# ScalarE takes over state copies, block copies, scaled products and gate biases in the mixers of a hybrid backbone block

## The chip, the cores and the metric

The kernel runs on one core of one Trainium2 chip. The metric is device microseconds of one execution, launch to end. Three runs of the kernel before gave a median of 1978.37 us (1975.06 to 1981.58).

Engines are named as the profile names them: PE is TensorE (PEld its weight loads), DVE is VectorE, ACT is ScalarE, POOL is GpSimd, SP issues most transfers. Each engine takes its instructions strictly in the order in which the program lists them for that engine, so an instruction that waits holds back all behind it on the same engine.

## The reference, cut to what matters

One layer, 256 latent tokens and 256 context tokens, width 2048, fp32. Each sequence is normalised and modulated, projected with `w_in`, and split into four head groups. Three of them are recurrences that run forward and backward; the context's end state starts the latent scan.

```
q, k = l2norm(q), l2norm(k)                                # GDN: 4 heads of 128
S_t = a_t (I - beta_t k_t k_t^T) S_{t-1} + beta_t k_t v_t^T ; o_t = S_t^T q_t
decay = exp(-c * sigmoid(w0 + tanh(w_lo) @ w2))            # RWKV-7: 8 heads of 64
a     = sigmoid(a0 + a_lo @ a2)
S_t = S_{t-1} (diag(w_t) - kk_t^T (a_t * kk_t)) + v_t^T k_t ; y_t = S_t r_t
```

The other two groups are GLA (a gated linear attention) and a short convolution. The four outputs are joined, multiplied by `w_out`, added to the stream; then a SwiGLU of width 5632 and a last RMSNorm on the latent tokens. The context goes through the mixers only, and of those through the recurrences' states only.

## The kernel before, in words

All is one core, four stages on the time axis of the profile:

- 0 to about 160 us: modulation vectors and the first projections (eleven tiles of `w_early`) for the context.
- about 160 to 1100 us: the mixers. The list `ORDER` names their pieces. Small letters are the context (`s == 0`), capitals the latent tokens (`s == 1`): `rw0` to `rw3` are RWKV head pairs (function `rwkv`, both directions `d`, so 16 unit passes in all), `gd0` to `gd3` are GDN heads (function `gdn`, eight passes), `gl` GLA pairs, `SC` short convolutions, and `pd`, `pr`, `pg` are projections whose results are parked in DRAM until a unit fetches them. Three further modulation vectors (`ada_pieces`, weights from `in_ada_later`) are fed in between the projections.
- about 1095 to 1240 us: `w_out` and the second norm. From there to the end: SwiGLU.

Every weight tile of a projection arrives as f32 (`wraw`). `split` makes from it a rounded part `wh` (ACT, line 197) and a rest `wl` (DVE, line 202); PE then multiplies three times (`wh` by the rounded activations, `wh` by their rest, `wl` by the rounded ones) into the PSUM tile `big`. The pool has three `wh` and three `wl`.

RWKV runs as stream "a", GDN and GLA as stream "b". Each unit pass has a front, a mid and a back part, and `in_parts` lets the front of the next pass run before the back of the last one. The two streams have PSUM tiles of their own: `ea` (two buffers) and `la` (one) for "a", `eb` (one) and `lb` (one) for "b".

The framework's planner works out, when the program is built, the order of instructions on each engine, from the order of the calls and from priorities: `tc.high_priority()` around a weight's load and split, and the offsets in `ORDER`. At run time that order is fixed.

The places that the change touches:

- `rw_gates` (line 837): two matmuls per pass (decay and `a`), each into an `ea` tile. DVE adds the bias and bounds from below by -87 in one instruction (line 847, recorded as helper line 208), into the halves of `rw_z`. ACT then makes the sigmoid of both halves in three instructions of 512 columns.
- `halves` (line 863): copies one block of 128 by 256 into a zero-filled block-diagonal tile `bd`, one instruction for each 64 partitions. `NB` and `KB` (from the two parts of `rw_BK`) go by DVE (line 873), `VB` by ACT (line 197).
- the state loop in the RWKV `back`: per chunk, PE forms `pS` and the output `po` in one `la` tile, and DVE multiplies `pS` by the chunk's decay into `rw_S` (helper line 206); for `d == 0` ACT copies `po`, for `d == 1` DVE adds it. There are 56 such states.
- GDN: the products `kk` and `kq` are copied out of an `eb` tile by DVE (lines 1145 and 1179); in `back`, each unit's product `pf` in the `lb` tile is scaled twice, by beta on ACT (`gd_Fb`, line 199) and by -beta exp(cum) on DVE (`gd_Fg`, line 206), two units per PSUM tile, and PE then multiplies with `gd_Fg`.

```
acopy(Fb[:, u]..., src, scale=sm["beta"][:, d, h, c:c + 1])
ts(Fg[:, u]..., src, sm["nbe"][:, d, h, c:c + 1], MUL)
```

Of the kernel before, what the change touches and what calls it, by code (L numbers as in the profile page):

```python
# [175 lines left out]
def block_kernel(ctx: ExitStack, tc: tile.TileContext, x, cx, ada_first, ada_later, ada_b, w_in, w_early, w_out,  # L176
# [63 lines left out]
    def pc(name, i=0, n=1, lo=0, hi=P):  # L240
        return par[lo:hi, POFF[name] + i:POFF[name] + i + n]
# [274 lines left out]
    with mix:  # L516
# [323 lines left out]
        def rw_gates(p, d, sm):  # L840

            z = mk(mx, [P, 2, T], "rw_z", 1)
            for i, n in enumerate(("w0", "a0")):
                pl = PB([P, T])
                w0 = i * 1024 + d * 512 + p * P
                mm(pl, sw[:, w0:w0 + P], sm["smd"][d])
                ts(z[:, i], pl, pc(n, d * 4 + p), ADD, -87.0, MAX)
            sigmoid(z.rearrange("p a t -> p (a t)"))
            cu = t1("rw_cu")
            runsum(cu, z[:, 0], d, z64)  # L850
            return cu, z[:, 1]
# [47 lines left out]
        def rwkv(p, s, raw, sm):  # L899
# [52 lines left out]
            def mid(d, v):  # L952
                cur[0] = "a"
                lo = 1 if d == 0 else 0
                KK, BK = v["KK"], v["BK"]
                NB, KB, VB = (r.next() for r in bd[1:])
                vv = t1("rw_v")
                shift(vv, com["v"], d * 12 + 8 + p, d)
                halves(NB, BK[:, :, 0, :], V)
                halves(KB, BK[:, :, 1, :], V)  # L960
                halves(VB, c64(vv), A)
                if s == 1:
                    r = t1("rw_r")
                    shift(r, com["r"], d * 12 + p, d)
                    IR = v["IR"] = mk(mx, [P, 4, 2, 64], "rw_IR", 1)
                    G.tensor_copy(IR[:, :, 0, :], bcast(istack, 1, 4))
                    tt(IR[:, :, 1, :], c64(r), v["ep"][:, :, lo:lo + 64], MUL)
                    rk = t1("rw_sq")
                    stt(rk, r, pc("rk", p), v["kp"], MUL, MUL)
                    pr = PB([P, T])  # L970
                    mm(pr, onesbd, rk)
                    if d == 0:
                        com["bonus"] = t1("rw_bonus")
                        tt(com["bonus"], pr, vv, MUL)
                    else:
                        tt(rk, pr, vv, MUL)
                        tt(com["bonus"], com["bonus"], rk, ADD, e=G)

                pv = PB([P, 4, P])
                for c in range(4):  # L980
                    TE.transpose(pv[:, c], f2(VB[:, c]), ident)
                v["vt"] = mk(mx, [P, 4, P], "rw_vt", 1)
                acopy(v["vt"], pv)

                pk = PB([P, 4, P])
                for c in range(4):
                    TE.transpose(pk[:, c], f2(KK[:, c]), ident)
                v["kt"] = mk(mx, [P, 4, P], "rw_kt", 1)
                acopy(v["kt"], pk)


                for t, tag in ((NB, "rw_na"), (KB, "rw_ka")):
                    pt, o = PB([P, 4, P]), mk(mx, [P, 4, P], tag, 1)
                    for c in range(4):
                        if s == 1:
                            mm(pt[:, c], f2(t[:, c]), f2(v["IR"][:, c]))
                        else:
                            TE.transpose(pt[:, c], f2(t[:, c]), ident)
                    if s == 1:
                        tt(o, pt, bcast(caus[d], 1, 4), MUL)  # L1000
                    else:
                        for hh in range(2):
                            sl = slice(64 * hh, 64 * hh + 64)
                            acopy(o[sl, :, :64], pt[sl, :, sl])
                    v[tag] = o

            def back(d, v):
                cur[0] = "a"
                w = P if s == 1 else 64
                LM, na, ka, kt_, vt = v["LM"], v["rw_na"], v["rw_ka"], v["kt"], v["vt"]  # L1010
                KH, EB = bdKh.next(), bdE.next()
                if s == 1 and d == 0:
                    com["y"] = t1("rw_y")
                F = mk(mx, [P, 4, P], "rw_F", 1)
                inverse(v["nL"], v["Xc"], (16, 32), [d == 0] * 4, na[:, :, :w], F[:, :, :w], w)
                pka = PB([P, 4, w], "l")
                for c in range(4):
                    mm(pka[:, c], LM[:, c, 1].rearrange("p h j -> p (h j)"), F[:, c, :w])
                for hh in range(2):
                    sl = slice(64 * hh, 64 * hh + 64)  # L1020
                    tt(KH[sl, :, hh, :], pka[sl, :, 0:64], ka[sl, :, 0:64], ADD)
                if s == 1:
                    Ah = mk(mx, [P, 4, 64], "rw_Ah", 1)
                    tt(Ah, pka[:, :, 64:P], ka[:, :, 64:P], ADD)
                pe = PB([P, 4, w], "l")
                for c in range(4):
                    mm(pe[:, c], kt_[:, c], F[:, c, :w])
                for hh in range(2):
                    sl = slice(64 * hh, 64 * hh + 64)
                    tt(EB[sl, :, hh, :], pe[sl, :, 0:64], bcast(istack[sl], 1, 4), ADD)  # L1030
                if s == 1:
                    Q = mk(mx, [P, 4, 64], "rw_Q", 1)
                    tt(Q, pe[:, :, 64:P], v["IR"][:, :, 1, :], ADD)
                S = get_state(("rw", p, d), f"rw_S{d}") if s == 1 else None
                order = (0, 1, 2, 3) if d == 0 else (3, 2, 1, 0)
                yc = c64(com["y"]) if s == 1 else None
                for n, c in enumerate(order):

                    pc_ = PB([P, 64 + P], "l")
                    po, pS = pc_[:, :64], pc_[:, 64:]  # L1040
                    if n < 3 or s == 0:
                        mm(pS, f2(KH[:, c]), vt[:, c], True, S is None)
                        if S is not None:
                            mm(pS, f2(EB[:, c]), S, False, True)
                    if s == 1:
                        mm(po, vt[:, c], Ah[:, c], True, False)
                        mm(po, S, Q[:, c], False, True)
                    if n < 3 or s == 0:
                        S = mk(mx, [P, P], f"rw_S{d}", 2)
                        ts(S, pS, v["dcol"][:, c:c + 1], MUL)  # L1050
                    if s == 1 and d == 0:
                        acopy(yc[:, c], po)
                    elif s == 1:
                        tt(yc[:, c], yc[:, c], po, ADD)
                if s == 0:
                    put_state(("rw", p, d), S)
                elif d == 1:
                    finale()
# [38 lines left out]
        def gdn(h, s, raw, sm):  # L1097
# [29 lines left out]
            def front():  # L1127
# [14 lines left out]
                    mm(pk[:, c], k[:, sl], k[:, sl])  # L1142
                kq = mk(mx, [P, 4, P], "gd_kq", 1)
                kk = kq[:, 0:2]
                V.tensor_copy(kk, pk)

                pbc = decays()
                dl = mk(mx, [P, 4, P], "gd_dl", 2)
# [12 lines left out]
            def mid():  # L1161
# [14 lines left out]
                    sl = slice(c * P, (c + 1) * P)  # L1176
                    mm(pk[:, c], k[:, sl], q[:, sl])
                kq = com["kq"][:, 2:4]
                V.tensor_copy(kq, pk)
                pbc = decays()  # L1180
                for d in range(2):
                    for c in range(2):
# [9 lines left out]
            def back():  # L1192
# [7 lines left out]
                for d in range(2):  # L1200
                    pf = PB([P, 2, 2, P], "l")
                    for c in range(2):
                        u = d * 2 + c
                        mm(pf[:, c].rearrange("p a b -> p (a b)")[:, :w], X[:, u],
                           R[:, u].rearrange("p a b -> p (a b)")[:, :w])
                    for c in range(2):
                        u = d * 2 + c
                        src = pf[:, c].rearrange("p a b -> p (a b)")[:, :w]
                        acopy(Fb[:, u].rearrange("p a b -> p (a b)")[:, :w], src, scale=sm["beta"][:, d, h, c:c + 1])
                        ts(Fg[:, u].rearrange("p a b -> p (a b)")[:, :w], src, sm["nbe"][:, d, h, c:c + 1], MUL)  # L1210
                    pe = PB([P, 2, 2, P])
                    for c in range(2):
                        u = d * 2 + c
                        mm(pe[:, c].rearrange("p a b -> p (a b)")[:, :w], tok[:, c],
                           Fg[:, u].rearrange("p a b -> p (a b)")[:, :w])
                    for c in range(2):
                        u = d * 2 + c
                        stt(EQ[:, u, 0], ident, sm["dec"][:, d, h, c:c + 1], pe[:, c, 0], MUL, ADD)
                        if s == 1:
                            tt(EQ[:, u, 1], pe[:, c, 1], com["qe"][:, d, c * P:(c + 1) * P], ADD)  # L1220
# [460 lines left out]
```

## Time and profile before

| | |
|---|---|
| median of three runs | 1978.37 us |
| the profiled execution's own time | 1979.17 us |
| its span, first to last instruction | 1977.4 us |
| mean granted TensorE clock | 0.983 |
| PE busy | 1858.0 us (94%) |
| DVE busy | 1352.5 us (68%) |
| ACT busy | 1020.7 us (52%) |
| POOL busy | 155.0 us (8%) |

Busy shares are of the span. A mean over the span mixes stages: the last 850 us are a dense product, while the mixers' stage has long chains over PE, DVE and ACT. What a row of idle time says is which instruction ended the wait of an engine.

### The profile page before, as it was taken

Reading aid. Unit: us, or ns where it says so; the run is one execution under the profiler, and the core shown is the slowest. Engines: PE = TensorE matmul, PEld = TensorE weight load, DVE = VectorE, ACT = ScalarE, POOL = GpSimd, SP = SyncE. Lnnn points to the kernel's source line nnn. Section 1 sums busy time; section 2 is a strip of 40 time slices with the busy share of each in tenths; the row PEclk is TensorE's granted clock in tenths of the full one; section 3 lists DMA queues with packets and bytes.
Section 4 is the critical chain, followed back from the end, with each engine's and each line's share of the span. In section 5 each row is a group of like instructions: output and inputs, shape, how many; then the busy total and the mean of one; then the engine's idle time right before and its main releaser. Section 6 shows DMA issues by size and latency. Waiting matters only on the chain.

```text
span 1977.4 us, 36172 instructions
## 1 busy us (share of the span) xinstructions
PE 1858.0 (94%) x13312; PEld 1622.9 (82%) x13312; DVE 1352.5 (68%) x3327; ACT 1020.7 (52%) x2125; POOL 155.0 (8%) x207
## 2 busy tenths in 40 slices
PE   5898899899999999999999998999999999999998
PEld 3777788788888988888999986888888888888886
DVE  3446767888879789899767567986555555555554
ACT  2225555575575655656455555555555545544444
POOL 0001000000001001101010001110010010000000
PEclk6999999899999999999999999999999999999999
DMA  8985877255473431322344665996555555665664
GB/s 332 397 341 199 277 244 238 69 190 176 126 240 106 146 100 61 101 72 86 110 142 143 220 185 173 318 316 212 184 189 184 189 185 187 201 207 193 193 196 153
DMA packets 162081, 374.66 MB, mean 189 GB/s; under 512 B 17896, under 2 KB 43752, under 8 KB 156784
## 3 DMA queue, kind: packets, MB, share of 16 engines
q1 hardware_dynamic: 156288, 368.21, 55.7%
q10 hardware_dynamic: 5616, 4.14, 0.7%
q8 instruction: 104, 1.70, 0.3%
q14 instruction: 73, 0.60, 0.1%
HBM read 360.48 MB, written 11.80 MB: 188 GB/s over the span
## 4 chain that ended last, share of the span: by engine, by line
PE 75%; DVE 9%; DMA 8%; ACT 5%; issue 2%; POOL 0%; SPq 0%; ACTq 0%; DVEq 0%; POOLq 0%
PE acc L214 40%; PE big L214 14%; PE la L214 6%; DMA wraw<-in_ada_later 5%; PE ea L214 5%; PE lb L214 3%; DVE wl L202 3%; PE eb L214 3%; PE ob L214 2%; ACT wh L197 2%; PE pt L214 0%; DMA wraw<-in_x 0%; DMA xin<-in_cx 0%; ACT rw_z L193 0%; DMA wraw<-in_w_in 0%
## 5 line engine op out<-in xcount | busy, mean ns | idle before, releaser
L202 DVE TENSOR_TENSOR wl<-wraw,wh 128x512 fp32r<-128x512 f32 x856 | 570.7, 693 | 370.0 <-ACT wh L197 364.0
L197 ACT ACTIVATE wh<-wraw 128x512 fp32r<-128x512 f32 x856 | 509.9, 625 | 485.9 <-PE acc L214 197.0
L214 PE MATMUL acc<-n,wh 128*128 128x512 f32 x1408 | 492.7, 398 | 3.3 <-ACT wh L197 3.3
L214 PE MATMUL acc<-n,wl 128*128 128x256 f32 x1408 | 383.2, 282 | 1.8 <-DVE wl L202 1.8
L214 PE MATMUL big<-nh,wh 128*128 128x256 f32 x1056 | 311.9, 296 | 4.4 <-ACT xs L197 3.0
L214 PE MATMUL big<-nh,wl 128*128 128x256 f32 x1056 | 311.2, 295 | 0.7 <-DVE wl L202 0.7
L214 PEld LDWEIGHTS acc<-n,wh 128*128 128x128 f32 x1408 | 259.4, 189 | 60.1 <-ACT wh L197 3.6
L214 PE MATMUL big<-nl,wh 128*128 128x256 f32 x1056 | 307.7, 292 | 0.0
L214 PEld LDWEIGHTS acc<-n,wl 128*128 128x128 f32 x1408 | 267.1, 190 | 11.7 <-DVE wl L202 3.3
L214 PEld LDWEIGHTS big<-nh,wh 128*128 128x128 f32 x1056 | 200.9, 190 | 11.3 <-ACT xs L197 3.8
L214 PEld LDWEIGHTS big<-nh,wl 128*128 128x128 f32 x1056 | 200.5, 190 | 4.0 <-issue 2.1
L214 PEld LDWEIGHTS big<-nl,wh 128*128 128x128 f32 x1056 | 200.8, 190 | 2.0 <-issue 1.1
L214 PE MATMUL acc<-wh,hH 128*128 128x512 f32 x352 | 137.6, 391 | 0.0
L214 PE MATMUL acc<-wh,hL 128*128 128x512 f32 x352 | 137.2, 390 | 0.0
L214 PE MATMUL acc<-wl,hH 128*128 128x512 f32 x352 | 137.2, 390 | 0.0
L202 POOL TENSOR_TENSOR hL<-sg,hH 128x256 fp32r<-128x256 f32 x44 | 46.7, 1061 | 452.5 <-ACT hH L197 452.5
L214 PEld LDWEIGHTS acc<-wh,hH 128*128 128x128 f32 x352 | 66.1, 188 | 14.1 <-ACT up L197 0.2
L214 PEld LDWEIGHTS acc<-wl,hH 128*128 128x128 f32 x352 | 66.1, 188 | 13.9 <-DVE wl L202 0.2
L214 PEld LDWEIGHTS acc<-wh,hL 128*128 128x128 f32 x352 | 66.1, 188 | 13.8
L214 PE MATMUL ob<-wraw,sc 128*32 128x128 f32 x1536 | 52.7, 280 | 24.9 <-DMA wraw<-in_ada_later 21.2
L214 PEld LDWEIGHTS ob<-wraw,sc 128*32 128x32 f32 x1536 | 39.9, 111 | 34.2 <-DMA wraw<-in_ada_later 27.6
L202 DVE TENSOR_TENSOR wl<-wr,wh 128x1408 fp32r<-128x1408 f32 x16 | 26.0, 1624 | 43.3 <-ACT wh L197 43.3
(482 smaller groups left out, 3175.3 us busy)
## 6 DMA issues: line engine op xcount, KB each, us to landing
wraw<-in_w_gu SPq DMA_DIRECT2D x174, 512.0 KB, 3.3
wraw<-in_w_in SPq DMA_DIRECT2D x264, 256.0 KB, 3.2
wraw<-in_ada_later SPq DMA_DIRECT2D x256, 256.0 KB, 4.2
wraw<-in_w_down SPq DMA_DIRECT2D x88, 512.0 KB, 4.2
ad<-in_ada_first SPq DMA_DIRECT2D x32, 1024.0 KB, 9.8
wraw<-in_w_out SPq DMA_DIRECT2D x64, 256.0 KB, 2.8
wr<-in_w_early SPq DMA_DIRECT2D x16, 704.0 KB, 6.2
xin<-in_cx SPq DMA_DIRECT2D x2, 1024.0 KB, 7.9
```

The costliest lines, as they stand in the source:

```text
L197: A.activation(o, i, AF.Copy)
L202: (e or V).tensor_tensor(out=o, in0=a, in1=b, op=op)
L214: return TE.matmul(o, l, r, start=start, stop=stop)
```

## The change

Five edits. RWKV's states, the `NB` and `KB` block copies, GDN's `gd_Fg` and its two product copies move from DVE to ACT with the same data. In the gates, ACT adds the bias (one instruction for each half, out of PSUM), and DVE bounds both halves at once, in place, in SBUF.

```diff
@@ rw_gates
                 mm(pl, sw[:, w0:w0 + P], sm["smd"][d])
-                ts(z[:, i], pl, pc(n, d * 4 + p), ADD, -87.0, MAX)
+                act(z[:, i], pl, AF.Identity, bias=pc(n, d * 4 + p))
+            ts(z.rearrange("p a t -> p (a t)"), z.rearrange("p a t -> p (a t)"), -87.0, MAX)
             sigmoid(z.rearrange("p a t -> p (a t)"))
@@ rwkv, mid
-                halves(NB, BK[:, :, 0, :], V)
-                halves(KB, BK[:, :, 1, :], V)
+                halves(NB, BK[:, :, 0, :], A)
+                halves(KB, BK[:, :, 1, :], A)
                 halves(VB, c64(vv), A)
@@ rwkv, back
                         S = mk(mx, [P, P], f"rw_S{d}", 2)
-                        ts(S, pS, v["dcol"][:, c:c + 1], MUL)
+                        acopy(S, pS, scale=v["dcol"][:, c:c + 1])
@@ gdn, front
-                V.tensor_copy(kk, pk)
+                acopy(kk, pk)
@@ gdn, mid
-                V.tensor_copy(kq, pk)
+                acopy(kq, pk)
@@ gdn, back
-                        ts(Fg[:, u]..., src, sm["nbe"][:, d, h, c:c + 1], MUL)
+                        acopy(Fg[:, u]..., src, scale=sm["nbe"][:, d, h, c:c + 1])
```

## Rows read from the trace of the kernel before

**Rows 1.** The page's chain that ended last, by engine, whole span.
```profile
PE 75%; DVE 9%; DMA 8%; ACT 5%; issue 2%; POOL 0%; SPq 0%; ACTq 0%; DVEq 0%; POOLq 0%
```

**Rows 2.** Busy time by stretch (columns: stretch, engines, PEclk, DMA share, GB/s).
```profile
200.00:1100.00 900.00, 842.49 (x7313) 769.07 (x7312) 730.69 (x2232) 520.13 (x1164) 74.14 (x114) 0.99 0.46 146
1100.00:1950.00 850.00, 840.33 (x4381) 714.85 (x4380) 517.29 (x865) 425.30 (x830) 65.88 (x60) 1.00 0.63 208
```

**Rows 3.** Waits of PE, 200 to 1100 us (total us, times, longest).
```profile
PE ob L214 <- DMA wraw<-in_ada_later: 18.2, 20, 1.9
PE ea L214 <- DVE rw_BK L202: 4.3, 5, 1.3
PE eb L214 <- DVE gd_Fg L206: 3.0, 4, 1.4
PE big L214 <- ACT xs L197: 3.0, 2, 1.5
...
PE lb L214 <- ACT gd_qe L197: 0.2, 1, 0.2
...
PE lb L214 <- DVE gd_qe L202: 0.2, 1, 0.2
```

**Rows 4.** DVE's instructions by form, 180 to 1095 us (count, busy, mean ns, idle before).
```profile
L206 DVE TENSOR_SCALAR rw_S<-la,rw_dcol 128x128 f32<-128x128 f32 x56 | 19.4, 347 | 9.3 <-PE la L214 8.8
L873 DVE COPY bd<-rw_BK 64x256 f32<-64x256 f32 x64 | 18.4, 287 | 1.4 <-PE ea L998 0.6
...
L208 DVE TENSOR_SCALAR rw_z<-ea,par 128x256 f32<-128x256 f32 x32 | 15.2, 480 | 5.6 <-PE ea L214 5.3
...
L206 DVE TENSOR_SCALAR gd_Fg<-lb,gnbe 128x256 f32<-128x256 f32 x16 | 7.7, 480 | 2.3 <-ACT gd_Fb L199 2.1
...
L206 DVE TENSOR_SCALAR gd_Fg<-lb,gnbe 128x128 f32<-128x128 f32 x16 | 5.5, 345 | 1.4 <-ACT gd_Fb L199 1.4
...
L1145 DVE COPY gd_kq<-eb 128x256 f32<-128x256 f32 x8 | 3.4, 419 | 0.4 <-PE eb L214 0.3
```

**Rows 5.** The second product copy, by its line (ns min/median/max).
```profile
L1179 DVE COPY gd_kq<-eb x4: 416/422/427, 638.1 to 984.2; 128x256 f32<-128x256 f32 x4
```

**Rows 6.** ACT's instructions by form, 180 to 1095 us (as rows 4).
```profile
L197 ACT ACTIVATE wh<-wraw 128x512 fp32r<-128x512 f32 x243 | 152.0, 627 | 108.6 <-PE big L214 93.4 <-DMA wraw<-in_w_in 6.3 <-DVE gd_Fg L202 2.5
...
L197 ACT ACTIVATE bd<-rw_v 64x256 f32<-64x256 f32 x30 | 12.3, 412 | 2.1 <-PE ea L981 1.6 <-DVE rw_v L211 0.2
...
L199 ACT ACTIVATE gd_Fb<-lb,gbeta 128x256 f32<-128x256 f32 x16 | 7.5, 472 | 11.3 <-PE lb L214 9.7 <-DVE gd_Fg L206 1.5
...
L199 ACT ACTIVATE gd_Fb<-lb,gbeta 128x128 f32<-128x128 f32 x16 | 5.8, 361 | 3.2 <-PE lb L214 2.3 <-DVE gd_Fg L206 0.8
...
L193 ACT ACTIVATE gd_silu<-eb,par 128x256 f32<-128x256 f32 x8 | 3.8, 473 | 6.0 <-PE eb L214 5.6 <-PE la L718 0.4
...
L197 ACT ACTIVATE gd_dl<-eb 128x256 f32<-128x256 f32 x4 | 1.5, 378 | 0.7 <-PE eb L1309 0.7
```

**Rows 7.** DVE's one-input instructions out of SBUF, at line 206 (as rows 5).
```profile
L206 DVE TENSOR_SCALAR gd_silu<-gd_c x20: 279/286/361, 185.0 to 936.2; 128x256 f32<-128x256 f32 x20
...
L206 DVE TENSOR_SCALAR gd_e<-gd_silu x4: 147/150/153, 401.6 to 546.5; 128x1 f32<-128x1 f32 x4
```

**Rows 8.** Timeline around one GDN scaling, 1001.4 to 1004.6 us (start, length, engine).
```profile
1001.83 0.47 ACT L199 ACTIVATE gd_Fb<-lb,gbeta 128x256 f32<-128x256 f32 x1 [1.28 <-PE lb L214]
...
1002.34 0.48 DVE L206 TENSOR_SCALAR gd_Fg<-lb,gnbe 128x256 f32<-128x256 f32 x1 [1.52 <-ACT gd_Fb L199]
...
1003.07 0.46 ACT L199 ACTIVATE gd_Fb<-lb,gbeta 128x256 f32<-128x256 f32 x1
...
1003.80 0.48 DVE L206 TENSOR_SCALAR gd_Fg<-lb,gnbe 128x256 f32<-128x256 f32 x1
```

**Rows 9.** Timeline of one gate pass, 904.2 to 909.6 us, DVE, then ACT.
```profile
905.24 0.48 DVE L208 TENSOR_SCALAR rw_z<-ea,par 128x256 f32<-128x256 f32 x1
...
906.41 0.63 ACT L193 ACTIVATE rw_z<-rw_z 128x512 f32<-128x512 f32 x1
```

**Rows 10.** Waits of ACT, 180 to 1095 us (as rows 3).
```profile
ACT wh L197 <- PE big L214: 93.4, 92, 3.1
```

More of the change, by code (lines that the diff above doesn't have):

```diff
@@ L1209, in back @@
                         acopy(Fb[:, u].rearrange("p a b -> p (a b)")[:, :w], src, scale=sm["beta"][:, d, h, c:c + 1])
-                        ts(Fg[:, u].rearrange("p a b -> p (a b)")[:, :w], src, sm["nbe"][:, d, h, c:c + 1], MUL)
+                        acopy(Fg[:, u].rearrange("p a b -> p (a b)")[:, :w], src, scale=sm["nbe"][:, d, h, c:c + 1])
                     pe = PB([P, 2, 2, P])
```

## The prediction

> **What bounds the kernel now.** Start with the stretches. All edits lie in RWKV and GDN units, which run between 181 and 1009 us, so the stage is the mixers', 200 to 1100 us. There PE is busy 842.5 of 900 us, DVE 730.7 (81%), ACT 520.1 (58%), POOL 74.1 [rows 2]. From 1100 us on PE is busy 840.3 of 850 us and none of the touched instructions is there, so that part stays as it is. What the stage can gain is bounded at first sight by PE's idle time, 900 - 842.5 = 57.5 us.
>
> Who ends that idle time is the next view, PE's waits. The rows there end in three kinds. Transfers of the modulation weights and of x: 18.2 us and one row of 1.8, together 20 us, which no edit touches. DVE: 19 rows from 4.3 us (`rw_BK`) down to 0.2, 22.4 us in sum. ACT: 13 rows from 3.0 us down to 0.2, 12.7 us in sum [rows 3]. The largest ACT row, 3.0 us, belongs to a tile of the latent norm, which isn't touched, so 9.7 us of ACT's can react.
>
> The chain of waits says the same of the whole span: PE 75%, DVE 9%, ACT 5% [rows 1]. So the stage is bound by PE's own work; DVE is the engine that makes it wait most often after the transfers, and ACT has more room than DVE.
>
> **The change part by part.** First what leaves DVE, by its rows [rows 4, 5]: 56 states 19.4 us, 64 block copies 18.4, 32 gate instructions 15.2, 32 `gd_Fg` 7.7 + 5.5, 12 product copies 3.4 + 4 x 0.422 = 5.1. Sum 71.3 us.
>
> What DVE gets: 16 bounds of 128 by 512 in SBUF. No row shows one. Of the same kind, 128 by 256 takes 286 ns and 128 by 1 takes 150 ns [rows 7], so 136 ns for 255 more columns; 512 columns give 286 + 137 = 0.42 us, estimated from these. From below it is 0.29 us (the 256 column row), from above 0.69 us (twice 347, the 128 column row out of PSUM). I take 0.42: 16 x 0.42 = 6.8 us (4.6 to 11). DVE's net: 71.3 - 6.8 = 64.5 us less, 730.7 to 666 us.
>
> What ACT gets, each by the ACT row of the same shape, source and kind of scale [rows 6]: states 56 x 0.361 = 20.2 (`gd_Fb` 128 by 128 out of PSUM with a scale per partition); block copies 64 x 0.412 = 26.4 (`VB`, the same copy); bias 32 x 0.473 = 15.1 (`gd_silu` out of `eb` with a bias per partition); `gd_Fg` 16 x 0.472 + 16 x 0.361 = 13.4; product copies 12 x 0.378 = 4.5. Sum 79.6 us, 520.1 to 600 us. After the change the two stand at 74% and 67% of the stage. Per instruction out of PSUM ACT and DVE cost the same (472 against 480 ns, 361 against 347); only the block copies out of SBUF are dearer, 412 against 287 ns.
>
> The Trainium skill, page "ScalarE: Activation LUTs", section "Rules for kernel authors", speaks against the change: adds, multiplies and bounds belong on VectorE, which it calls up to about three times as fast per element in bf16. The trace agrees with that for the 64 copies in SBUF alone, and by the smaller ratio just given; for the fp32 instructions out of PSUM it shows no advantage. Three times the price for all that moves would put some 214 us on ACT in place of 79.6; no row supports that.
>
> How engine time turns into PE's idle time isn't in any row, since these engines mostly work behind PE's cover (PE fills with projections). My estimate is that what waits for an engine grows as its busy time over its free time. DVE: 730.7/169.3 = 4.3 becomes 666/234 = 2.85, a factor of 0.66; 22.4 us x 0.34 = **7.6 us gained**. ACT: 520/380 = 1.37 becomes 600/300 = 2.0, a factor of 1.46; 9.7 us x 0.46 = **4.5 us lost**. Bounds: the DVE share gains nothing or all 22.4 us; the ACT share loses nothing, or the 12 us of the second rival.
>
> Single chains. *GDN's scaling*: `gd_Fb` and `gd_Fg` read one PSUM tile and already run one after the other: 1001.83 ACT, 1002.34 DVE (waiting for ACT), 1003.07 ACT, 1003.80 DVE until 1004.28, so 2.45 us with gaps in which each engine takes other work [rows 8]. On one engine they are 4 x 0.47 = 1.9 us at most. That is 0.55 us less on 16 chains, 9 us, and PE is seen waiting for `gd_Fg` for 3.0 us [rows 3]; a third of it is in the DVE term, of the rest I take **1.5 us gained** (0 to 2). DVE also stops standing idle for them (2.3 + 1.4 us [rows 4]).
>
> *Gates*: now the second DVE instruction starts at 905.24, ends at 905.72, and the exponential starts at 906.41 when ACT is free [rows 9]. After, ACT does two instructions, then DVE 0.42 us behind whatever its queue holds, then ACT again; queued behind the exponential are other ACT work and the scan on DVE. I take the bound and about another half microsecond for the second crossing: 0.9 us on 16 passes, 14 us of chain. PE is idle 57.5/900 = 6.4% of the stage, so 6.4% of it shows: **0.9 us lost** (nothing to 14 if nothing covers it).
>
> *States*: 347 to 361 ns, 56 times, 0.8 us of chain, and DVE no longer stands 9.3 us for them [rows 4]; for `d == 0` the output copy is behind the state on one engine where it was behind it across two. *Block copies*: 64 x 0.125 = 8 us more engine time, before transposes that wait for other tiles too. *Product copies*: 40 ns shorter each. These three at nothing, as PE's projections cover them; without that cover the first two cost 0.8 and 8 us.
>
> No transfer is added. The eight writes of a context state to DRAM are issued on ACT's queue already, right behind the state, which is now on the same engine.
>
> Sum: -7.6 + 4.5 - 1.5 + 0.9 = **-3.7 us**, from the profiled execution's 1979.2 to 1975.5; the median of the runs lies 0.8 us lower, so 1974.7, rounded to 1974. Late next, where DVE's stalls go, are the transfers' 20 us and ACT's queue.
>
> **The rivals.** *First: DVE is what really paces the stage.* PE's idle rows understate it if PE filled waits with projections that are then missing later. For it: DVE is 9% of the chain, 178 us, and 81% busy in the stage. Against: PE is 94% busy there, and part of those 178 us lies in other stages. If all of them shrink as DVE's work in the stage does, by 64.5/730.7 = 8.8%, that is -16 us: 1962.
>
> *Second, on the other side: ACT's queue holds the states back.* ACT stands 108.6 us in front of `wh`, of that 93.4 us in 92 waits of 1.0 us mean until PE frees a weight buffer [rows 6, 10], 108.6/900 = 12% of the stage. Each moved instruction may be queued behind such a wait. For the 56 states, 32 `gd_Fg` and 16 gates, 104 in all, 12% x 1.0 us = 12.5 us, if PE has nothing else: 1990. It decides when the waits on ACT for states, gates and `gd_Fg` that PE is seen to pay exceed the 9 us that DVE's relief and the single chains give back. Against: the planner puts `wh` where it expects the buffer free, and PE has projections ready at most times. The Trainium skill's rule above would point the same way.
>
> *Third: nothing net.* The planner draws up a new order with the new engines and both effects go under PE's cover; the time stays at 1978. This is the lower end of the likeliest case, and I count it there.
>
> **How the numbers follow.** About 0.3%, 6 us, is what a measurement of this kernel can tell from no change (its three runs lie 6.5 us apart). Likeliest, 0.50: a net of a few microseconds, the sum above, own range 1966 to 1979; of this 0.17 is faster by over 0.3% and 0.33 within. First rival 0.22: 0.21 faster, 0.01 within. Second rival 0.28: 0.24 slower, 0.04 within. So faster 0.38, same 0.38, slower 0.24. The order of all engines is drawn up anew, which spreads each case by several microseconds: the range reaches from 6 us past the first rival, 1956, to just past the second, 1992.
>
> **What would show it.** In 200 to 1100 us: DVE busy near 666 us, ACT near 600. On ACT, states at 0.36 us, block copies at 0.41, biases at 0.47; on DVE 16 bounds at 0.42. PE's waits ended by DVE near 15 us, those ended by ACT near 17, the row for `gd_Fg` near 1. Four GDN scalings in a row within 1.9 us. If the mixers' stage ends more than 10 us earlier with DVE rows gone from the chain, the first rival is right; if rows of PE waiting for `rw_S`, `gd_Fg` or `rw_z` on ACT pass 10 us, the second. The prediction is wrong altogether if the stage from 1100 us on changes its length, or if the transfers' 20 us move by more than the terms here.

## The result, and the profile after

The changed kernel took 1987.48 us (median of five runs, 1984.65 to 1993.71); the kernel before, in the same rounds, 1975.06 us (1972.02 to 1981.58). The ratio is 1.006 with a 95% interval of 1.0043 to 1.0077. A second comparison with ten runs (e8_after_again, below) gave 1.0041 (1.0026 to 1.0057). So the change costs about half a per cent, 8 to 12 us, where a gain of 3.7 us was forecast. The profiled execution took 1984.65 us, its span is 1982.8 us and its mean granted clock 0.991.

Busy time by stretch, the kernel after, columns as in [rows 2]:

```profile
200.00:1100.00 900.00, 841.48 (x7270) 763.58 (x7271) 685.71 (x2052) 580.53 (x1351) 77.32 (x113) 0.99 0.46 144
1100.00:1950.00 850.00, 840.32 (x4398) 714.86 (x4398) 517.43 (x865) 423.94 (x826) 66.34 (x60) 0.99 0.63 208
```

The later stretch is as it was, to 0.01 us of PE time. In the mixers' stage DVE is busy 45.0 us less and ACT 60.4 us more. PE's idle time has hardly grown (58.5 against 57.5 us), but PE began 7270 matmuls in it where it had begun 7313: the loss doesn't stand in the column of idle time. Part of it is counted as busy: over the whole span the same matmuls are busy 1861.1 us where they were 1858.0.

The moved instructions and two of DVE's that wait for ACT's results, 180 to 1095 us, columns as in [rows 4]; first ACT, then DVE:

```profile
L197 ACT ACTIVATE bd<-rw_BK 64x256 f32<-64x256 f32 x64 | 26.5, 414 | 5.3 <-DVE rw_BK L211 4.2 <-DVE rw_BK L202 0.3
...
L199 ACT ACTIVATE rw_S<-la,rw_dcol 128x128 f32<-128x128 f32 x56 | 20.3, 363 | 18.7 <-PE la L214 18.2
...
L193 ACT ACTIVATE rw_z<-ea,par 128x256 f32<-128x256 f32 x31 | 14.4, 471 | 10.4 <-PE ea L214 7.4 <-DVE rw_bonus L202 2.8
...
L199 ACT ACTIVATE gd_Fg<-lb,gnbe 128x256 f32<-128x256 f32 x16 | 7.6, 474 | 0.0
...
L199 ACT ACTIVATE gd_Fg<-lb,gnbe 128x128 f32<-128x128 f32 x16 | 5.9, 372 | 0.0
...
L197 ACT ACTIVATE gd_kq<-eb 128x256 f32<-128x256 f32 x12 | 4.5, 379 | 6.7 <-PE eb L214 6.7
```

```profile
L202 DVE TENSOR_TENSOR wl<-wraw,wh 128x512 fp32r<-128x512 f32 x238 | 164.9, 695 | 67.7 <-ACT wh L197 59.3 <-PE lb L214 1.7 <-PE big L214 1.2
...
L206 DVE TENSOR_SCALAR rw_z<-rw_z 128x512 f32<-128x512 f32 x16 | 7.6, 478 | 11.7 <-ACT rw_z L193 11.6
```

The moved instructions last as long as forecast from ACT's own rows, within 11 ns; only the bound, estimated at 0.42 us, takes 0.48. What is new stands in the last columns: ACT now stands 18.7 us at the head of its queue in front of the states, 10.4 in front of the biases, 6.7 in front of the product copies and 5.3 in front of the block copies, 41 us in which everything behind them stands too. Other stands of ACT shrank by more: all its waits in 200 to 1100 us sum to 373.0 us before and 311.3 after. And DVE stands 11.7 us in front of its new bounds, until ACT has made the biases.

The waits of DVE in 200 to 1100 us, before and after (total us, times, longest):

```profile
DVE wl L202 <- ACT wh L197: 40.5, 61, 2.3
DVE rw_S L206 <- PE la L214: 8.8, 12, 1.8
...
DVE rw_z L208 <- PE ea L214: 5.3, 8, 2.6
```

```profile
DVE wl L202 <- ACT wh L197: 55.7, 71, 2.7
DVE rw_z L206 <- ACT rw_z L193: 11.6, 8, 3.5
```

All DVE waits that ACT ends sum to 76.3 us before (29 rows) and 116.9 us after (29 rows): 40.6 us more. That this is near the 45.0 us by which DVE's work shrank shows no cause: in 900 us that PE paces, work that leaves DVE must come back as idle time of DVE. What the rows add is whom DVE waits for in it: the waits that PE ends stayed (68.1 and 67.3 us), those that ACT ends grew.

The waits of PE, the rows that answer to [rows 3]:

```profile
PE ob L214 <- DMA wraw<-in_ada_later: 19.1, 20, 1.9
PE ea L214 <- DVE rw_BK L202: 6.8, 6, 2.0
PE eb L214 <- DVE gd_q L211: 3.9, 4, 1.4
PE lb L214 <- DVE ivbW L202: 3.7, 5, 1.2
...
PE la L214 <- ACT rw_S L199: 1.1, 3, 0.7
...
PE eb L214 <- ACT gd_Fg L199: 0.7, 2, 0.5
```

By engine: those that DVE ends 22.4 before, 25.9 after; those that ACT ends 12.7 and 11.6. The wait for `gd_Fg`, which the prediction named, did fall, from 3.0 to 0.7 us.

A second measure shows the rest. It takes the distance from each matmul's start to the next one's, between 160 and 1130 us, subtracts the usual distance of that shape, and adds up what is left by the matmul that comes late (us; worked out from the traces of three kernels without the edits and four with them, all described below):

```
late matmul            before, e9, e10      after, e8, e11, e12
la<-rw_vt,bdKh         7.2  6.4  6.3        11.5 11.5 10.6 12.2    opens a state's step
ea<-rw_BK,bd           9.4  9.6  8.4        11.2 12.1 18.0 15.8
la<-ivaX,ivaW          2.9  1.4  3.6         6.6  7.4  5.6  4.4
lb<-ivbX,ivbW          5.9  4.3  5.3         7.9  7.9  6.5  7.6
all                  247.9 244.8 244.3     254.6 256.1 256.2 258.3
```

The four edited kernels lose 7 to 14 us in this stage. The four rows shown grow by some 16 us on average, others shrink; all four are short chains that go from engine to engine (state step, block transposes, the inversions).

### The profile page after: what moved, and what is told of

Same layout as the page of the kernel before. It is cut to its first block, busy times and chain, and to the rows that moved or that the text cites. A ratio compares the mean times of both kernels' runs of the same rounds, so it can differ in the third digit from the quotient of the medians.

```text
span 1982.8 us, 36211 instructions
## 1 busy us (share of the span) xinstructions
PE 1861.1 (94%) x13311; PEld 1620.6 (82%) x13312; DVE 1309.4 (66%) x3147; ACT 1085.3 (55%) x2321; POOL 158.9 (8%) x207
## 4 chain that ended last, share of the span: by engine, by line
PE 59%; DVE 5%; ACT 3%; DMA 3%; issue 1%; POOL 1%; SPq 0%; DVEq 0%; POOLq 0%; ACTq 0%
PE acc L214 36%; PE big L214 10%; PE ea L214 4%; PE la L214 4%; PE lb L214 2%; PE eb L214 2%; DVE wl L202 1%; DMA wraw<-in_ada_later 1%; ACT wh L197 1%; ACT rw_z L193 0%; DVE ivaXc L202 0%; DVE ivaw L202 0%; PE ob L214 0%; DMA xr_r_k<-xs 0%; DMA rw_rraw<-xr_r_r 0%
## 5 line engine op out<-in xcount | busy, mean ns | idle before, releaser
L214 PEld LDWEIGHTS acc<-wl,hH 128*128 128x128 f32 x352 | 66.1, 188 | 13.9 <-DVE wl L202 0.2
L214 PEld LDWEIGHTS ob<-wraw,sc 128*32 128x32 f32 x1536 | 40.0, 111 | 36.0 <-DMA wraw<-in_ada_later 29.4
```

The costliest lines, as they stand in the source:

```text
L214: return TE.matmul(o, l, r, start=start, stop=stop)
```

## The experiments

Theory at the start: the moved instructions are paid in ACT's queue (the second rival). Rival: the planner's new order, not the instructions, is what costs. Later a third question: load on ACT, or lateness of the results.

**One part at a time, order drawn up by the planner.** Each has one piece of the diff alone:

```diff
e1  -ts(z[:, i], pl, pc(...), ADD, -87.0, MAX)   +act(z[:, i], pl, AF.Identity, bias=pc(...)); ts(z, z, -87.0, MAX)
e2  -halves(NB/KB, ..., V)                       +halves(NB/KB, ..., A)
e3  -ts(S, pS, dcol, MUL)                        +acopy(S, pS, scale=dcol)
e4  -ts(Fg, src, nbe, MUL); V.tensor_copy(kk/kq) +acopy(Fg, src, scale=nbe); acopy(kk/kq, pk)
```

> Only the gates' edit: 32 biases on ScalarE, 16 joint bounds on VectorE; the other four edits undone. Two theories. Order: the whole change moved some 200 instructions, so the planner drew up another order of all engines, and that order, not the price of a moved instruction, costs the 0.6%; then each edit alone gives a shift of its own of up to some 10 us of either sign, and the four shifts do not add up to the +12 us of the whole. Price: one edit puts work or a crossing on the path; the gates are the only edit that adds a crossing (VectorE between two ScalarE steps), so this kernel alone should be slower by most of the 12 us (1983 to 1988), with PE waiting longer for rw_BK.

Measured 1980.79 us, ratio 1.0009 (0.9992 to 1.0026).

> Only the 64 block copies move to ScalarE (0.285 to 0.414 us each, 8 us of engine time more). Order: a shift of either sign, unrelated to those 8 us. Price: if ScalarE's time is what counts, this edit has the largest share of it (26 of 80 us) and should be slower by 4 to 8 us, with PE's waits for rw_na and rw_ka longer.

Measured 1983.97 us, ratio 1.0025 (1.0005 to 1.0044).

> Only RWKV's 56 states move to ScalarE. Order: a shift of either sign. Price (ScalarE's queue holds the states behind a wait for a weight buffer, the second rival of the prediction): slower by about 56/104 of 12.5 us, 7 us, with PE waiting on ScalarE's rw_S for several us.

Measured 1980.67 us, ratio 1.0012 (0.9993 to 1.0030).

> Only GDN's 32 scaled products and 12 product copies move to ScalarE. The four scalings in a row take 1.6 us in place of 2.7 in the trace of the whole change, so by the prediction's own terms this is the edit that should gain: 1 to 3 us faster. Order: a shift of either sign that may hide that. Price: 32/104 of 12.5 us slower, 4 us.

Measured 1986.10 us, ratio 1.0034 (1.0020 to 1.0048).

No part shows a gain; the first and the third can't be told from no change. GDN's part, forecast to gain on its own chain, costs most, though its four scalings did get shorter. The four sum to 0.80%; with an error of some 0.35% that can't be told from the whole.

**Is it the order?** e5 makes all edits but holds PE to the order of the kernel before; e6 is the kernel before with PE held to the order of the kernel after. e7 is an edit the other way, planner's order.

```diff
+    for a, b in zip(order[:-1], order[1:]):        # e5, e6: PE's list of the other kernel
+        tc.add_manual_dep(pe_seq[int(b)], pe_seq[int(a)].name, ...)
-                halves(VB, c64(vv), A)             # e7
+                halves(VB, c64(vv), V)
```

> All five edits, but TensorE is held to exactly the order of its 10888 instructions that the planner gave the kernel before (the edits change none of them, only their order: 4719 of 10888 places differ). VectorE and ScalarE run the changed instructions. If the order that the planner drew up anew for TensorE costs the 0.6%, this kernel is within 0.2% of the kernel before (1976 to 1983 beside 1979), or a few us faster, as the prediction's sum said of the instructions themselves. If the price of the moved instructions on ScalarE costs it, this one is as slow as the whole change, +8 to +14 us.

Measured 2002.10 us, ratio 1.0124 (1.0104 to 1.0143).

> The other half of the cross: no edit at all, every instruction on its old engine, but TensorE held to the order that the planner gave the changed kernel. If order costs the 0.6%: +6 to +14 us. If the moved instructions cost it: no change, within 0.2%. If both orders are made for their own instructions, each misfit is slower than its own: then this one and the other half both lose.

Measured 2040.55 us, ratio 1.0332 (1.0308 to 1.0356).

> The kernel before with one edit in the opposite direction: the 32 VB block copies go from ScalarE to VectorE (4040 of TensorE's 10888 places differ by it). If ScalarE's load is what costs, this is faster by 32 x 0.41 us of ScalarE time, some 2 to 5 us by the slopes of the four single edits. If any new order of the planner loses against the one of the kernel before, it is slower by 2 to 7 us like the four single edits.

Measured 1986.99 us, ratio 1.0051 (1.0031 to 1.0070).

An order of PE that was made for other engines' work costs up to 3.3%: orders and instructions belong together, so neither run says what the new order costs by itself. e7 moves work the other way, off ACT, and loses as well, as much as the whole change: under a newly drawn order `VB` on DVE is no gain. So "more work on ACT costs" doesn't explain all of these runs.

**How far do redrawn orders scatter?** The same kernels with one priority changed, which redraws all orders and edits nothing:

```diff
-    "... PD1:150 RW1 FF0:-100 ..."       +    "... PD1:150 RW1:50 FF0:-100 ..."     e9 (before), e11 (after)
-    "GD1 RW2 PD2:-1100 ..."              +    "GD1:100 RW2 PD2:-1100 ..."           e10 (before), e12 (after)
```

> The whole change once more beside the others on one chip, as the measure for them: +0.4% to +0.8% by the first measurement, whatever the theory.

Measured 1985.82 us, ratio 1.0041 (1.0026 to 1.0057).

> No instruction of the kernel before is changed; in its list of pieces RW1 becomes RW1:50, a small priority offset, so the planner draws up another order (2386 of TensorE's 10888 places differ). If the order of the kernel before is one that any redrawing loses against, +2 to +10 us. If redrawing shifts the time by chance to both sides, within -8 to +8 us. If order hardly matters unless it misfits, within 0.15%.

Measured 1978.65 us, ratio 1.0006 (0.9989 to 1.0023).

> As the run above, with GD1:100 in place of GD1 (2022 places differ). Same three expectations; two such kernels tell a systematic loss from chance better than one.

Measured 1973.58 us, ratio 0.9979 (0.9963 to 0.9996): the fastest version of all that ran.

> All five edits and RW1:50 (2058 places of TensorE's order differ from the changed kernel's). If the price of the moved instructions costs the 0.4 to 0.6%, any sensible order keeps it: +6 to +14 us. If the drawn order costs it, another one gives another time: the two kernels with new offsets lie several us apart from the changed kernel, and one of them may fall to the kernel before or below.

Measured 1988.88 us, ratio 1.0051 (1.0032 to 1.0070).

> All five edits and GD1:100 (1188 places differ). As the run above.

Measured 1988.20 us, ratio 1.0051 (1.0036 to 1.0066).

Three orders with the edits lie at 1.0041 to 1.0060, three without at 0.9979 to 1.0006. The scatter of an order is about a fifth of a per cent; the edits cost more under each, and with the same offset 0.45% (e11 against e9) and 0.72% (e12 against e10). So the loss isn't the luck of one drawn order. One rival stays untested: apart from these two offsets, the list `ORDER` is the one of the kernel before in every run, and no run chooses offsets for the changed kernel.

**The edits with every engine's order held.** All five engines keep the order of the kernel before; the moved instructions are put into ACT's list at the time at which DVE made them in the trace before, the bounds 0.6 us behind the last gate instruction that they replace. Edits as above: all (e13), states (e14), GDN (e15), block copies (e16).

```diff
+    traced = [i for i in nc.cur_bb.bb.instructions]
+    for held in ORDERS:                            # one list for each engine
...
+        for a, b in zip(order[:-1], order[1:]):
+            tc.add_manual_dep(traced[int(b)], traced[int(a)].name, ...)
```

> All five edits, and nothing drawn up anew: PE, POOL and SyncE keep the order of the kernel before to the last instruction, VectorE keeps its order less the 196 instructions that leave it, and ScalarE keeps its own with those 196 put in where the trace of the kernel before has them on VectorE (each bound 0.6 us after the last gate instruction it replaces). So engines change, neighbours do not. If the planner's new order costs the 0.4 to 0.6%, this one is within 0.15% of the kernel before or faster (the prediction's sum for the instructions themselves was -3.7 us). If the moved instructions themselves cost it (longer in ScalarE's queue, behind its waits for weight buffers), it stays at +6 us or more.

Measured 1994.01 us, ratio 1.0089 (1.0063 to 1.0115).

> As the run above with the states alone (56 instructions). Order: within 0.15% of before. Price: +3 us or more, since the matmul that opens a state step waited 10 to 11 us in sum in every trace with the states on ScalarE and 6 to 7 us in those without.

Measured 1980.57 us, ratio 1.0022 (1.0007 to 1.0037).

> As above with GDN's scaled products and product copies alone (44 instructions). With the planner's own order this edit lost 0.34%. Order: 0 to -3 us, since the four scalings in a row get shorter (2.7 to 1.6 us). Price: +4 us or more.

Measured 1982.85 us, ratio 1.0041 (1.0022 to 1.0060).

> As above with the 64 block copies alone, the only edit whose instructions are clearly dearer on ScalarE (0.285 to 0.414 us). With the planner's own order it lost 0.25%. Order: within 0.15%. Price: +3 us or more.

Measured 1982.12 us, ratio 1.0023 (1.0005 to 1.0040).

Holding the order doesn't bring the gain: e13 costs 0.89%. Whether the planner's new order (0.41 to 0.60%) wins some of that back isn't clear, as most of the intervals overlap. The three parts sum to 0.86%, with an error of some 0.3%, so what is left for the gates can't be told. No run holds the kernel before to its own order; that holding adds no work is seen in e16, which leaves 36171 instructions in its trace where the kernel before leaves 36172.

Since PE makes the same 13312 matmuls in the same order in these kernels, each can be set against its like in the kernel before. e13 is 13.0 us late at 1100 us, near the 13.9 us between the profiled executions (1993.07 and 1979.17); of it 6.0 us arise in front of the matmul that reads `gd_Fg` (3.4 us in e15) and 2.0 in front of the one that opens a state's step (1.6 in e14). The other three rows of the table above don't grow in it (-0.5, 0.0 and -0.5 us). Its stage, its waits of PE and its waits of DVE:

```profile
200.00:1100.00 900.00, 834.47 (x7219) 758.08 (x7220) 681.01 (x2041) 574.47 (x1339) 74.55 (x115) 0.99 0.46 144
```

```profile
PE ob L599 <- DMA wraw<-in_ada_later: 16.2, 18, 2.6
PE eb L599 <- ACT gd_Fg L584: 7.8, 9, 1.6
PE ea L599 <- DVE rw_BK L587: 4.2, 5, 1.3
```

```profile
DVE wl L587 <- ACT wh L582: 51.2, 62, 3.0
DVE rw_z L591 <- ACT rw_z L578: 14.7, 9, 3.9
```

PE's waits that ACT ends sum to 26.1 us, 13.4 more than before; those that DVE ends to 18.8, 3.6 fewer. `gd_Fg` alone went from 3.0 us in 4 waits on DVE [rows 3] to 7.8 in 9 on ACT. DVE stands for ACT 123.4 us in all, 47 more than before.

The largest piece, `gd_Fg`, belongs to the places that the run gives the moved instructions, and isn't what the change itself pays. One chain of e13 on ACT (start, length, engine):

```profile
874.54 0.47 ACT L584 ACTIVATE gd_Fb<-lb,gbeta 128x256 f32<-128x256 f32 x1 [1.22 <-PE lb L599]
...
876.18 0.47 ACT L584 ACTIVATE gd_Fg<-lb,gnbe 128x256 f32<-128x256 f32 x1
...
877.59 0.47 ACT L584 ACTIVATE gd_Fb<-lb,gbeta 128x256 f32<-128x256 f32 x1
...
878.40 0.47 ACT L584 ACTIVATE gd_Fg<-lb,gnbe 128x256 f32<-128x256 f32 x1
```

Between the four scalings of the 16 chains lie 54 other ACT instructions in e13, 7 in the changed kernel. The chains sum to 46.8 us in e13 and 45.1 in e15, where the kernel before takes 42.9 and the change 25.5. So e13 too is an order made for other engines' work, as e5 is, and its 0.89% is the price of the edits at these places.

The traces of the parts say less than their ratios. At 1100 us e16 is 0.9 us early; all of the 3.7 us that it is late at the end arise after that. e14 is 5.3 us late there, but between 320 and 340 us alone it falls back by 8.1 us, and e15, 7.3 us late, falls back by 5.3 between 320 and 350. Within these stretches the granted clock falls to the lower of its two levels (1.2 GHz); in e14 PE had been busy 6.50 of the 10 us before. The kernel before at the same place, then e14, columns as in [rows 2]:

```profile
330.00:344.00 14.00, 13.64 (x156) 11.89 (x156) 7.83 (x18) 6.34 (x15) 0.24 (x1) 1.00 0.69 222
330.00:344.00 14.00, 14.00 (x97) 13.27 (x89) 3.53 (x8) 3.44 (x8) 0.00 (x0) 0.51 0.40 129
```

The kernel before has such stretches elsewhere, and its mean granted clock goes from 0.982 to 0.993 over its 28 executions beside these runs; that this stretch comes from the edit isn't shown.

**Load or lateness?** e17 makes 174 of the 196 moved instructions on both engines, ACT's results unused; e18 the same with DVE's results unused. All orders are held.

```diff
+    def both(o, i, s, real): ...                   # j: a spare 8-bit tile
+        vo, ao = (j, o) if real == 1 else (o, j)   # e17: real = 0, e18: real = 1
+        ts(vo, i, s, MUL)
+        acopy(ao, i, scale=s)
```

> The kernel before with every engine's order kept, and 174 of the 196 moved instructions also made by ScalarE, at the places that they have in e13_all_fixed, into a spare 8-bit tile that nobody reads; VectorE still makes the results that are used (20 block copies and 2 product copies are not doubled, and there is no bound). So ScalarE's load is that of the change and nothing else is changed but that a PSUM buffer is freed only when both engines have read it. e13_all_fixed cost 0.89%. If what is paid is that the moved results themselves come late out of ScalarE's queue, this run stands at 1.000 to 1.003 of before. If what is paid is that ScalarE's other work is pushed back by the load (the prediction's ACT term, 4.5 us, grown), it stands at 1.006 to 1.009. By the prediction's own ACT term it would be 1.0023.

Measured 2015.02 us, ratio 1.0176 (1.0152 to 1.0200).

> e13_all_fixed (all edits, every engine's order kept), but VectorE still makes 174 of the 196 moved instructions too, at their old places, into a spare 8-bit tile that nobody reads: the change without the relief of VectorE. What e13_all_fixed (1.0089) lies below this run is what the relief is worth. If the relief is worth nothing, this run stands at 1.007 to 1.011; if it is worth the 7.6 us of the prediction's DVE term, at 1.011 to 1.015; by the first rival's 16 us at 1.017. The difference between this run and e17_act_load is what it costs that the results come from ScalarE and no longer from VectorE, with both engines loaded alike, the 16 bounds included: about nothing if the load alone decides, 0.5% to 0.9% if lateness of the results decides.

Measured 2021.79 us, ratio 1.0204 (1.0178 to 1.0230).

Both are above all that was expected, and the trace of e17 shows one reason: the doubled instruction has a wait of its own.

```profile
ACT dump L590 <- DVE rw_S L597: 30.0, 34, 2.8
...
ACT dump L590 <- DVE gd_Fg L597: 8.4, 17, 1.0
```

ACT stands 30.0 us for DVE in front of the spare states, which DVE doesn't write: the two engines' reads of one PSUM tile are put one after the other. That goes with the Trainium skill, page "PSUM — Partial Sum Buffer", section "PSUM bank collisions raise a hardware error", by which two engines mustn't be in the same 32 partitions of one bank at once, reads included. The pair therefore doesn't separate load from lateness, and that stays open. What it does bound: e18 lies 1.15% above e13 (2.04 against 0.89), so DVE's relief is worth at most those 23 us when the order is held; how much of them is the added wait isn't separated.

## Why the prediction was wrong

**The step that failed** is the sum of the two engine terms, "7.6 us gained" for DVE and "4.5 us lost" for ACT, and in it the DVE term first of all. In the four traces with the edits and an order of the planner's (after, e8, e11, e12), PE's waits that DVE ends sum to 25.9, 26.7, 29.4 and 24.0 us; in the three without (before, e9, e10) to 22.4, 25.6 and 20.2. On average that is 3.8 us more where 7.6 fewer were forecast. Those that ACT ends sum to 11.6, 12.4, 13.5 and 14.6 against 12.7, 11.2 and 11.6: 1.2 us more where 4.5 were forecast. So the two terms cost 5.0 us where a gain of 3.1 stood. The rest of the 8 to 12 us is in no row of PE's waits; the second measure finds 7 to 14 us, the waits included, as late matmuls, much of it in short chains that the sum put at nothing or had no term for. With the order held (e13) DVE's waits are 3.6 us fewer and ACT's 13.4 more, but 3.0 of the 3.6 are only the `gd_Fg` row, which ACT now ends: on all else DVE's relief is worth 0.6 us there.

The time itself, 1987.48 us, lies inside the range of 1956 to 1992, on the side to which the prediction gave 0.24.

*Why the DVE term didn't come.* It took DVE's busy share for the cause of PE's waits. But much of what DVE does waits for ACT's results: `wl` needs `wh`, the bound needs the bias, `rw_y` the state. DVE's work fell 45.0 us, and its waits that ACT ends rose from 76.3 to 116.9 us (e8, e11 and e12: 115.5, 120.6 and 121.8 us; unedited e9 and e10: 78.8 and 78.5), while PE's waits for DVE didn't fall. That DVE waits more for ACT with the edits is shown, under held and redrawn orders; that this is why PE's waits for DVE stayed, and how much of the loss on PE each wait makes, is not.

*Why the ACT term was off.* The second rival had the side and nearly the time (1990 against 1987), its mechanism only in part, so the nearness is partly luck. Its price of a wait came from ACT's stands in front of `wh`, and these fell from 93.4 us [rows 10]:

```profile
ACT wh L197 <- PE big L214: 80.2, 75, 3.5
```

What arose are stands in front of the moved instructions themselves, 41 us, which the working asked about for the gates alone: for states and scalings it named what would be queued in front of them, not what would be queued behind. The sign that the prediction set for this rival, over 10 us of PE waits for `rw_S`, `gd_Fg` and `rw_z`, isn't met after (1.8 us); in e13 the three rows sum to 9.1.

*The single chains.* GDN's scaling went as described. One of them, the kernel after, ACT (start, length, engine), to be set against [rows 8]:

```profile
1002.53 0.47 ACT L199 ACTIVATE gd_Fb<-lb,gbeta 128x256 f32<-128x256 f32 x1 [0.49 <-PE lb L214]
1002.90 0.47 ACT L199 ACTIVATE gd_Fg<-lb,gnbe 128x256 f32<-128x256 f32 x1
1003.25 0.47 ACT L199 ACTIVATE gd_Fb<-lb,gbeta 128x256 f32<-128x256 f32 x1
1003.61 0.64 ACT L197 ACTIVATE wh<-wraw 128x512 fp32r<-128x512 f32 x1
1004.13 0.48 ACT L199 ACTIVATE gd_Fg<-lb,gnbe 128x256 f32<-128x256 f32 x1
```

Even with a `wh` between, the four take 2.1 us; all 16 take 25.5 us where they took 42.9. PE's wait for `gd_Fg` fell by 2.3 us, so the 1.5 us stand as far as that row goes; yet e4, which has this part alone, loses 0.34%. A reading that no run tests: the shorter chain takes ACT in one piece, and the other stream's work stands behind it.

*Gates.* From the last matmul to the first exponential it takes 1.57 us on average where it took 1.41, so 2.6 us over 16 passes instead of 14; e1 measures 0.09%, within its error. That is within the range given, and near the 0.9 us taken.

*States and block copies at nothing, "as PE's projections cover them".* e14 and e16 measure 0.22% and 0.23%, some 4 us each; the price given for lost cover was 0.8 and 8 us. For the states, late matmuls of 1.6 to 2.0 us at the head of a step back it; for the block copies the trace of e16 shows no loss in the stage, so whether the cover failed there is open.

*The Trainium skill's rule* (page "ScalarE: Activation LUTs", section "Rules for kernel authors") pointed the right way, that such work stays on VectorE, but not for its reason: a state takes 363 ns on ACT against 347 on DVE [rows 4], and an instruction three times dearer appears nowhere here.

The third rival, nothing net, is excluded by the interval of the ratio, and so is the first, 1962.

## What to carry to other kernels

The duration of an instruction alone doesn't price its move to another engine. List, for each moved instruction, how long the engine will stand at the head of its queue for the producer, and which other engines' work comes out of that queue. Ask of the relieved engine what it waits for: here it did less and waited more for the engine that took its work, and PE's waits for it didn't fall. To test such a move, redraw the order of both kernels a few times and compare the two groups: that separates the edits from the luck of one plan. Holding every engine's order lets one set matmul against matmul, but the places that it gives the moved instructions are part of what it measures, and a stretch at the lower clock can be most of a difference between two traces.

## What was not expected of the hardware

- Neighbouring instructions of one engine overlap. In the timeline of the kernel after, three that last 0.47 us start 0.37 and 0.35 us apart. So durations overstate occupancy: the moved instructions sum to 79.2 us on ACT, and its busy time rose 60.4 us in 200 to 1100 us, 64.6 over the whole span; DVE was to lose 64.5 us by durations and lost 45.0 and 43.1.
- A held order that doesn't fit the other engines costs PE 3.3% (e6) with not one instruction changed.
